# Up projections of two MLPs: two of four pairs of input row tiles by seven products of sums

## The chip, the cores and the metric

The kernel runs on one core of one Trainium2 chip. The metric is the device time in microseconds (us) of one execution, for fixed inputs of the sizes below. Outputs are compared with the reference's.

## The reference

A two-layer trunk over 1056 frames: 1024 of a new stream (the prompt) and 32 of a running one (the sample). The model width is 1024, the MLP's is 4096, and all data are float32.

```
for i in range(2):
    a = rmsnorm(h, norm_mix[i])
    y = hgrn2_mixer(a, ...) if i == 0 else short_conv_mixer(a, ...)
    h = h + y
    m = rmsnorm(h, norm_mlp[i])
    h = h + square(relu(m @ w_up[i])) @ w_down[i]     # (1056,1024)@(1024,4096), (1056,4096)@(4096,1024)
return rmsnorm(h, norm_final), states
```

The change is in the MLP, in the output projections of the two mixers ahead of it (`y @ w_out`, 1024 by 1024) and in how the weights of the conv mixer are cut.

## The kernel before, in words

Data lie transposed: the 1024 channels as eight tiles of 128 partitions by 1056 tokens (`hT[0]` to `hT[7]`). Every float32 operand is split into a high part (a cast to the matmul's fp32r, on ScalarE: `xh`, `whi`) and a low part (the operand less its high part, on VectorE: `xl`, `wlo`). A product is three matmuls, low by high, high by low and high by high (`mm3`), into one PSUM sum. A scale of a norm is applied where a product is read (`nrm.r`, made by `Norm.scale` with nine VectorE operations over 1056 columns, `rsqrt`), the norm's vector where the operand is split.

An MLP runs over 16 chunks of 256 of its 4096 columns:

- `up(c, 0)` and `up(c, 1)` make the chunk's two row tiles `u`: eight input tiles, tokens in groups of 384, 384 and 288, three matmuls each: 72 matmuls a stage. VectorE reads PSUM by relu times scale (L787), ScalarE squares (L788).
- `sums(c)` takes the two tiles `u` as a matrix of two by two blocks (two row tiles by two halves of 528 tokens) and makes from it seven factors B11, Q1, Q2, B22, T3, B21, T4 (`xsums`): four sums and differences on VectorE, each factor with a high part on ScalarE and a low part on VectorE.
- `down(c, 0)` and `down(c, 1)` multiply these by seven factors of the down weights A11, S1, S2, S4, S3, A12, A22, for two pairs `p` of output tiles each: seven products of two by two blocks where plain multiplication has eight. A product is six matmuls of 264 columns (three, by two quarters of the tokens); a stage is 7 x 2 x 6 = 84 matmuls (L812). S1 to S4 are sums of weight blocks, made by four additions on POOL in the raw tile (L720), after A11, A12 and A22 have been cast from it. Products gather in PSUM banks named a, b and c, and each gathered value is also added to the right half of an `hT` tile: by VectorE (L821), and in steps 0 and 6 (`STAGED`) by a copy to SBUF on ScalarE (`st`, L708) and an addition on POOL (L709). A bank is used again after it is read.

The stages come as up(c,0), up(c,1), down(c-1,0), down(c-1,1), sums(c). The weights of a stage are loaded and cut two stages ahead. Within that, a scheduler sets each engine's own order; an engine does its list strictly in that order. PSUM has four tiles (`pb`) of two banks. In layer 1 the last two chunks are multiplied plainly at the end (`groups`), in layer 0 the last one (`plain`).

Where the words below speak of a chunk, it is one up part and two down stages: in the steady part of the trace one follows the other every 43.9 us.

Of the kernel before, what the change touches and what calls it, by code (L numbers as in the profile page):

```python
# [8 lines left out]
F32 = mybir.dt.float32  # L9
# [26 lines left out]
def trunk_kernel(  # L36
# [21 lines left out]
    xs = ctx.enter_context(tc.tile_pool(name="xs", bufs=1))  # L58
    ws = ctx.enter_context(tc.tile_pool(name="ws", bufs=4))
    fp = ctx.enter_context(tc.tile_pool(name="fp", bufs=18))  # L60
    pj_cm = tc.tile_pool(name="pj", bufs=3, space=PSUM)
# [13 lines left out]
    xh = [xs.tile([P, NTOK], F32R, tag=f"xh{k}", name=f"xh{k}") for k in range(KT)]  # L75
    xl = [xs.tile([P, NTOK], F32R, tag=f"xl{k}", name=f"xl{k}") for k in range(KT)]
# [509 lines left out]
    for steps in late:  # L586
        steps()
    hp_cm.__exit__(None, None, None)
    for k in range(KT):
        split(k, heads[k].Y)  # L590
    rc_cm.__exit__(None, None, None)
    pj_cm.__exit__(None, None, None)


    mp = ctx.enter_context(tc.tile_pool(name="mp", bufs=1, reuse_waits="tile"))
    pb = ctx.enter_context(tc.tile_pool(name="pb", bufs=4, space=PSUM, reuse_waits="tile"))

# [10 lines left out]
    def mm_block(ps, n, c0, wt, j, srcs, kk0=0):  # L608
        nk = len(srcs)
        cs = slice(j * P, (j + 1) * P)  # L610
        for k in range(nk):
            hi, lo = wt[(kk0 + k) // 4]
            kk = (kk0 + k) % 4
            ah, al = srcs[k]
            mm3(ps[:, :n], hi[:, kk, cs], lo[:, kk, cs], ah[:, c0 : c0 + n], al[:, c0 : c0 + n],
                k == 0, k == nk - 1)

    def mm_rows(pss, wt, j, srcs, mid=None):

        cs = slice(j * P, (j + 1) * P)  # L620
        nk = len(srcs)
        for k in range(nk):
            hi, lo = wt[k // 4]
            ah, al = srcs[k]
            if mid and k == nk - 1:
                mid()
            for g in range(3):
                sl, n = gsl(g)
                mm3(pss[g][:, :n], hi[:, k % 4, cs], lo[:, k % 4, cs], ah[:, sl], al[:, sl], k == 0, k == nk - 1)

    xsrc = [(xh[k], xl[k]) for k in range(KT)]
    hT = [None] * KT

    class Norm:


        def __init__(self):
            self.acc = mp.tile([P, NTOK], F32, tag="acc", name="acc")
            self.n = 0

        def add(self, m):
            if self.n == 0:
                nc.scalar.activation(self.acc, hT[m], AF.Square)
            else:
                sq = mp.tile([P, NTOK], F32, tag="sq", name="sq")
                nc.scalar.activation(sq, hT[m], AF.Square)
                nc.gpsimd.tensor_tensor(self.acc, self.acc, sq, op=ALU.add)
            self.n += 1

        def scale(self):  # L650
            v = mp.tile([P, NTOK], F32, tag="sq", name="nv")
# [10 lines left out]
    def out_proj(W, first):  # L662

        nrm = Norm()
        for m2 in range(4):
            wt = wload(W, m2)
            for j in range(2):
                m = 2 * m2 + j
                if first:
                    hT[m] = ft(f"hT{m}")  # L670
                    nc.gpsimd.dma_start(out=hT[m], in_=x_t[m * P : (m + 1) * P, :])
                _, pss = trio()
                if m in (0, KT - 1):
                    mm_rows(pss, wt, j, xsrc)
                for g in range(3):
                    sl, n = gsl(g)
                    ps = pss[g]
                    if 0 < m < KT - 1:
                        mm_block(ps, n, sl.start, wt, j, xsrc)
                    nc.vector.tensor_tensor(hT[m][:, sl], hT[m][:, sl], ps[:, :n], op=ALU.add)  # L680
                nrm.add(m)
        return nrm

    def split_h(k, vcol):
        split(k, hT[k], scale=vec[:, vcol + k : vcol + k + 1])
# [10 lines left out]
    WAT = {"A11": (0, 0), "A12": (0, 1), "A22": (0, 2), "S2": (1, 0), "S4": (1, 1), "S1": (1, 2), "S3": (1, 3)}  # L696
# [4 lines left out]

    TO = (((0, 0, ALU.add),), ((1, 1, ALU.subtract),), ((0, 1, ALU.add),), ((0, 1, ALU.add),),
          ((1, 1, ALU.subtract),), ((0, 0, ALU.add),), ((1, 0, ALU.subtract),))
    q2 = lambda t: t.rearrange("p (i c) -> p i c", i=2)
    STAGED = (0, 6)

    def stage(d, st, v, op):
        nc.scalar.copy(q2(st), v)  # L708
        nc.gpsimd.tensor_tensor(d, d, st, op=op)  # L709

    def wsums(src):

        raw, hi, lo = wtiles()
        hi2 = ws.tile([P, 4, 256], F32R, tag="whi", name="whi")
        lo2 = ws.tile([P, 4, 256], F32R, tag="wlo", name="wlo")
        nc.sync.dma_start(out=raw, in_=src)
        nc.scalar.copy(hi[:, :3], raw[:, :3])
        nc.vector.tensor_tensor(lo[:, :3], raw[:, :3], hi[:, :3].bitcast(F32), op=ALU.subtract)  # L718
        for d, o in ((2, 3), (3, 0), (0, 2), (1, 0)):
            nc.gpsimd.tensor_tensor(raw[:, d], raw[:, d], raw[:, o], op=ALU.add)  # L720
        nc.scalar.copy(hi2, raw)
        nc.vector.tensor_tensor(lo2, raw, hi2.bitcast(F32), op=ALU.subtract)
        ts = ((hi, lo), (hi2, lo2))

        def at(f, p):
            t, i = WAT[f]
            return [x[:, i, p * P : (p + 1) * P] for x in ts[t]]

        return at

    def xsums(u0, u1):
# [4 lines left out]
        def part(f, src, neg=False):  # L736
            t = fp.tile([P, 2, HALF], F32R, tag="ft", name=f)
            h, l = t[:, 0], t[:, 1]
            if neg:
                nc.scalar.activation(h, src, AF.Copy, scale=-1.0)  # L740
                nc.vector.scalar_tensor_tensor(l, src, -1.0, h.bitcast(F32), op0=ALU.mult, op1=ALU.subtract)
            else:
                nc.scalar.copy(h, src)
                nc.vector.tensor_tensor(l, src, h.bitcast(F32), op=ALU.subtract)
            X[f] = (h, l)

        add = lambda d, a, b, op: nc.vector.tensor_tensor(d, a, b, op=op)
        part("B11", b11)
        part("B22", b22)
        add(b22, b12, b22, ALU.subtract)  # L750
        add(b12, b11, b12, ALU.subtract)
        add(b11, b22, b11, ALU.subtract)
        part("Q1", b12)
        part("Q2", b11)
        part("T3", b22, True)
        part("B21", b21)
        add(b21, b11, b21, ALU.add)
        part("T4", b21, True)
        return X

    def mlp(layer, nrm, on_final, last):
        Wu, Wd = wg_up[layer], wg_down[layer]
        U, X = {}, {}
        two = lambda t: t[:, :768].rearrange("p (i c) -> p i c", i=2)
        sq = lambda t: nc.scalar.activation(t, t, AF.Square)

        def up(c, j):
            m = 2 * c + j

            def run(wt):  # L770
# [357 lines left out]
```

## Time and profile before

| what | value |
|---|---|
| time, median of 3 runs | 2445.47 us (2443.81 to 2446.0) |
| the profiled execution | 2445.29 us, span 2443.6 us, granted clock 0.995 |
| busy TensorE, VectorE, ScalarE, GpSimd | 2412.2, 1635.0, 775.8, 744.1 us |
| HBM traffic | 114 MB read, 5 MB written, 49 GB/s |
| HGRN mixer up to its output projection | 0 to 527 us of the span |
| output projection, MLP of layer 0 | 527 to 620, 620 to 1343 us |
| conv mixer, MLP of layer 1 | 1343 to 1710, 1710 to 2443 us |

PE is TensorE's matmuls, PEld its weight loads, DVE VectorE, ACT ScalarE, POOL GpSimd. A row of the timeline has the start, the length, the engine, the line, output and inputs with their shape, how many instructions stand together, and in brackets the idle time before them and what ended it. A row of the chain of waits has the start, the length, and the engine, tile and line. A row of a group has the busy time and the mean length of one instruction in ns. Lines are those of the kernel before.

### The profile page before, as it was taken

What the parts mean: (1) busy time and instruction counts of PE and PEld (TensorE: products, weight loads), DVE (VectorE), ACT (ScalarE), POOL (GpSimd) and SP (SyncE); (2) the same over time, 40 slices, a digit from 0 to 9 for tenths busy, and PEclk for the clock granted to TensorE, in tenths of its full rate; (3) what the DMA queues carried; (4) which work ended last, traced back from release to release, by engine and by line L of the source; (5) the groups of instructions that cost most, each with busy time, mean ns of one, the idle gap of its engine ahead of it and who ended that gap; (6) DMA issues with size and microseconds to landing.
All of it is one profiled execution on the core that took longest, in us unless ns stands there. A gap on an engine that the chain in (4) does not pass through costs nothing.

```text
span 2443.6 us, 39446 instructions
## 1 busy us (share of the span) xinstructions
PE 2412.2 (99%) x16548; PEld 2373.4 (97%) x16548; DVE 1635.0 (67%) x2384; ACT 775.8 (32%) x1275; POOL 744.1 (30%) x792
## 2 busy tenths in 40 slices
PE   8999999999999999999999999999999999999998
PEld 8999999989999999999999999999999999999997
DVE  8776666652887787877868533343877877868765
ACT  5121212122433334333335111023334333333334
POOL 3110100102244453444545000002253444534423
PEclk9999999999999999999999999999999999999999
DMA  4101010121011111111111111111111111111111
GB/s 151 39 21 56 22 56 22 56 91 52 28 60 44 45 51 44 61 44 44 53 44 54 42 52 44 43 53 36 41 47 44 61 44 44 53 44 61 44 35 71
DMA packets 35760, 121.99 MB, mean 50 GB/s; under 512 B 4336, under 2 KB 7552, under 8 KB 35584
## 3 DMA queue, kind: packets, MB, share of 16 engines
q1 hardware_dynamic: 33632, 113.58, 14.4%
q0 software_dynamic: 1952, 5.92, 0.7%
q8 instruction: 129, 2.11, 0.4%
q14 instruction: 47, 0.39, 0.1%
HBM read 114.09 MB, written 5.39 MB: 49 GB/s over the span
## 4 chain that ended last, share of the span: by engine, by line
PE 97%; DVE 2%; ACT 0%; issue 0%; DMA 0%; DVEq 0%; SPq 0%; ACTq 0%
PE pb L812 25%; PE pb L108 17%; PE pb L109 17%; PE pb L110 17%; PE pj L108 4%; PE pj L109 4%; PE pj L110 3%; PE v L492 1%; PE v L493 1%; PE v L494 1%; PE aps L385 1%; PE aps L390 1%; PE ops L427 1%; PE ups L402 1%; PE ops L426 1%; PE aps L388 0%
## 5 line engine op out<-in xcount | busy, mean ns | idle before, releaser
L108 PE MATMUL pb<-xh,wlo 128*128 128x384 f32 (+1 forms) x2544 | 829.3, 326 | 3.4 <-DVE hT L838 3.4
L109 PE MATMUL pb<-xl,whi 128*128 128x384 f32 (+1 forms) x2544 | 822.4, 323 | 0.0
L110 PE MATMUL pb<-xh,whi 128*128 128x384 f32 (+1 forms) x2544 | 822.4, 323 | 0.0
L709 POOL TENSOR_TENSOR hT<-hT,st 128x528 f32<-128x528 f32 x232 | 373.2, 1635 | 404.0 <-ACT st L708 404.0
L108 PEld LDWEIGHTS pb<-xh,wlo 128*128 128x128 f32 x2544 | 478.6, 188 | 8.2 <-issue 2.5
L110 PEld LDWEIGHTS pb<-xh,whi 128*128 128x128 f32 x2544 | 478.7, 188 | 0.4
L109 PEld LDWEIGHTS pb<-xl,whi 128*128 128x128 f32 x2544 | 478.7, 188 | 0.2
L821 DVE TENSOR_TENSOR hT<-hT,pb 128x528 f32<-128x528 f32 x580 | 383.4, 697 | 9.1 <-PE pb L812 0.8
L720 POOL TENSOR_TENSOR raw<-raw 128x256 f32<-128x256 f32 x232 | 209.7, 904 | 336.5 <-DVE wlo L718 322.8
L94 ACT CAST whi<-raw 128x1024 fp32r<-128x1024 f32 (+1 forms) x143 | 149.0, 1044 | 454.9 <-PE pb L110 268.0
L95 DVE TENSOR_TENSOR wlo<-raw,whi 128x1024 fp32r<-128x1024 f32 (+1 forms) x143 | 202.6, 1420 | 67.4 <-ACT whi L94 66.9
L812 PE MATMUL pb<-B,whi 128*128 128x264 f32 x1392 | 226.8, 285 | 0.0
L812 PEld LDWEIGHTS pb<-B,whi 128*128 128x128 f32 x1392 | 193.2, 189 | 0.0
L108 PE MATMUL pj<-xh,wlo 128*128 128x384 f32 (+1 forms) x536 | 177.7, 332 | 7.1 <-ACT xh L183 7.1
L109 PE MATMUL pj<-xl,whi 128*128 128x384 f32 (+1 forms) x536 | 173.4, 323 | 0.0
L110 PE MATMUL pj<-xh,whi 128*128 128x384 f32 (+1 forms) x536 | 173.1, 323 | 0.0
L787 DVE SCALAR_TENSOR_TENSOR u<-pb,nr 128x768 f32<-128x768 f32 x120 | 82.2, 704 | 124.0 <-PE pb L110 124.0
L708 ACT COPY st<-pb 128x528 f32<-128x528 f32 x232 | 133.0, 600 | 80.6 <-PE pb L812 68.9
L812 PE MATMUL pb<-T,whi 128*128 128x264 f32 x928 | 150.9, 284 | 0.0
L812 PE MATMUL pb<-Q,whi 128*128 128x264 f32 x928 | 150.7, 284 | 0.0
L812 PE MATMUL pb<-B,wlo 128*128 128x264 f32 x696 | 144.6, 289 | 3.3 <-DVE hT L821 3.3
L788 ACT ACTIVATE u<-u 128x768 f32<-128x768 f32 (+1 forms) x128 | 81.7, 642 | 161.3 <-DVE u L787 156.4
(243 smaller groups left out, 3620.3 us busy)
## 6 DMA issues: line engine op xcount, KB each, us to landing
raw<-in_wg_up_dram SPq DMA_DIRECT2D x64, 512.0 KB, 3.5
raw<-in_wg_down_dram SPq DMA_DIRECT2D x64, 512.0 KB, 3.5
raw<-in_wg_in_hgrn_dram SPq DMA_DIRECT2D x31, 512.0 KB, 4.3
raw<-in_wg_cu_conv_dram SPq DMA_DIRECT2D x16, 512.0 KB, 3.5
xk<-in_x_t_dram SPq DMA_DIRECT2D x8, 528.0 KB, 8.6
hT<-in_x_t_dram POOLq DMA_DIRECT2D x8, 528.0 KB, 7.3
raw<-in_wg_out_hgrn_dram SPq DMA_DIRECT2D x8, 512.0 KB, 4.1
raw<-in_wg_b_conv_dram SPq DMA_DIRECT2D x8, 512.0 KB, 3.6
```

Source lines behind the costliest of these rows:

```text
L94: nc.scalar.copy(hi, raw)
L95: nc.vector.tensor_tensor(lo, raw, hi.bitcast(F32), op=ALU.subtract)
L108: nc.tensor.matmul(ps, wlo, ah, start=start, stop=False)
L109: nc.tensor.matmul(ps, whi, al, start=False, stop=False)
L110: nc.tensor.matmul(ps, whi, ah, start=False, stop=stop)
L708: nc.scalar.copy(q2(st), v)
L709: nc.gpsimd.tensor_tensor(d, d, st, op=op)
L720: nc.gpsimd.tensor_tensor(raw[:, d], raw[:, d], raw[:, o], op=ALU.add)
L787: nc.vector.scalar_tensor_tensor(d, ps, 0.0, rr, op0=ALU.max, op1=ALU.mult)
L788: nc.scalar.activation(u[:, sl], u[:, sl], AF.Square)
L812: nc.tensor.matmul(t[:, q, :QT], wf, xf[:, q * QT : (q + 1) * QT], start=start and n == 0, stop=n == 2, skip_group_check=True)
L821: nc.vector.tensor_tensor(q2(d), q2(d), v, op=op)
```

## The change

The up projection of a chunk becomes one stage `up(c)`. Input row tiles 0 to 3 are taken as two pairs, and each pair's product with the chunk's two output tiles goes by seven products, as the down stages do it; tiles 4 to 7 stay plain, in halves of 528 tokens. The stage is 7 x 2 x 6 + 4 x 4 x 6 = 180 matmuls of 264 columns. Its list is `PAIR`: the bank, the two factors (or the output tile and half, for the plain products) and the name of the read that follows. Eight reads of PSUM gather the four blocks of `u` in SBUF: the first of a block is a copy by ScalarE or, for the last block, a read by VectorE together with the scale; the others are additions on VectorE. The second output tile is made with its sign turned (`op0` is min, and its plain weights are scaled by -1). The first chunk of a layer uses the order `LATE`, with the norm's scale made ahead of its step 10, and scales after all reads.

The up weights come as two tiles of 1024 columns (`wpair`): one is cut as the down weights are, with four additions on POOL, one into two plain parts. Weight parts are tiles of 512 columns, six for the high and six for the low parts, where there were four of 1024; raw tiles are two, not three. The factors of the input tiles are made once a layer: `hsums` in `out_proj`, after output tiles 3 and 5. They share the tiles of `xh` and `xl` or lie in six tiles `e`. The staged copies of the down stages have two tiles, not four.

```diff
-    def out_proj(W, first):
+    def out_proj(W, first, xsrc, vcol):
...
+            if m in (3, 5):
+                X = hsums(m // 2 - 1, X, vcol)
+        X["rows"] = [parts(hT[k], vec[:, vcol + k : vcol + k + 1]) for k in range(4, KT)]
+        return nrm, X
...
-    WAT = {"A11": (0, 0), "A12": (0, 1), "A22": (0, 2), "S2": (1, 0), "S4": (1, 1), "S1": (1, 2), "S3": (1, 3)}
+    WAT = {"A11": (0, 0), "A12": (0, 2), "A22": (1, 0), "S1": (2, 0), "S3": (2, 2), "S2": (3, 0), "S4": (3, 2)}
...
     def wsums(src):
 
-        raw, hi, lo = wtiles()
-        hi2 = ws.tile([P, 4, 256], F32R, tag="whi", name="whi")
-        lo2 = ws.tile([P, 4, 256], F32R, tag="wlo", name="wlo")
-        nc.sync.dma_start(out=raw, in_=src)
-        nc.scalar.copy(hi[:, :3], raw[:, :3])
-        nc.vector.tensor_tensor(lo[:, :3], raw[:, :3], hi[:, :3].bitcast(F32), op=ALU.subtract)
+        raw = wraw(src)
+        t = lambda i: raw[:, i * 256 : (i + 1) * 256]
+        hl = [wpart(raw[:, :512]), wpart(t(2))]
         for d, o in ((2, 3), (3, 0), (0, 2), (1, 0)):
-            nc.gpsimd.tensor_tensor(raw[:, d], raw[:, d], raw[:, o], op=ALU.add)
-        nc.scalar.copy(hi2, raw)
-        nc.vector.tensor_tensor(lo2, raw, hi2.bitcast(F32), op=ALU.subtract)
+            nc.gpsimd.tensor_tensor(t(d), t(d), t(o), op=ALU.add)
+        hl += [wpart(raw[:, 512:]), wpart(raw[:, :512])]
...
+    def mm_half(ps, wt, x, start, stop):
+        hi, lo = wt
+        for n, (w, v) in enumerate(((lo, x[0]), (hi, x[1]), (hi, x[0]))):
+            for q in range(2):
+                nc.tensor.matmul(ps[:, q, :QT], w, half(v, q), start=start and n == 0, stop=stop and n == 2,
+                                 skip_group_check=True)
+    PAIR = (("a", ("A11", "B11"), "a1"), ("b", ("S1", "Q1"), "b1"), ("c", ("A12", "B21"), None), ("c", (0, 0), "c"),
+            ("a", ("S2", "Q2"), "a2"), ("d", (1, 1), "d"), ("a", ("S3", "T3"), "a3"), ("b", ("S4", "B22"), None),
+            ("b", (0, 1), "b2"), ("a", ("A22", "T4"), None), ("a", (1, 0), "a4"))
+    LATE = (0, 1, 4, 7, 6, 2, 9, 3, 8, 10, 5)
+    def wpair(src):
+        at = wsums(src[0])
+        raw = wraw(src[1])
+        return at, wpart(raw[:, :512]), wpart(raw[:, 512:], -1.0)
...
+    READ = {"a1": (0, 0), "c": (0, 0), "a2": (0, 1), "b2": (0, 1), "b1": (1, 1), "a3": (1, 1), "d": (1, 1), "a4": (1, 0)}
...
+                    if b in made:
+                        nc.vector.tensor_tensor(q2(d), q2(d), ps, op=ALU.add)
+                    elif left[b] or c == 0:
+                        nc.scalar.copy(q2(d), ps)
+                    else:
+                        src = ps
+                    made.add(b)
+                    if not left[b]:
+                        r = lambda: nrm.r[:, sl]
+                        def end():
+                            if src is d:
+                                nc.vector.scalar_tensor_tensor(d, d, 0.0, r(), op0=op0, op1=ALU.mult)
+                            else:
+                                nc.vector.scalar_tensor_tensor(q2(d), src, 0.0, q2(r()), op0=op0, op1=ALU.mult)
+                            nc.scalar.activation(d, d, AF.Square)
+                        later.append(end) if c == 0 else end()
```

How the change moves instructions is seen in the order of three engines. The number behind a name tells tiles of one name apart; `st` is a staged copy, `raw` a weight tile as loaded, `pb` a PSUM tile.

GpSimd (POOL), in a steady part of layer 0, the two down stages before the next up stage. Before, the last six staged additions of the pair of downs, and the weights' additions (of the down stages of the next chunk) behind them:

```order
L709 TENSOR_TENSOR hT1_5399<-hT1_5399,st_21448 128x528
L709 TENSOR_TENSOR hT3_5575<-hT3_5575,st_21457 128x528
L709 TENSOR_TENSOR hT4_5669<-hT4_5669,st_21473 128x528
L709 TENSOR_TENSOR hT6_5845<-hT6_5845,st_21483 128x528
L709 TENSOR_TENSOR hT5_5751<-hT5_5751,st_21566 128x528
L709 TENSOR_TENSOR hT7_5927<-hT7_5927,st_21575 128x528
L720 TENSOR_TENSOR raw_21603<-raw_21603 128x256 x4
```

Now, the same six (L894) with the four additions of the next up stage's weights, raw_12478 (L740), in between:

```order
L894 TENSOR_TENSOR hT1_5427<-hT1_5427,st_12610 128x528
L894 TENSOR_TENSOR hT3_5611<-hT3_5611,st_12619 128x528
L740 TENSOR_TENSOR raw_12478<-raw_12478 128x256
L894 TENSOR_TENSOR hT4_5732<-hT4_5732,st_12651 128x528
L740 TENSOR_TENSOR raw_12478<-raw_12478 128x256
L894 TENSOR_TENSOR hT6_5945<-hT6_5945,st_12661 128x528
L740 TENSOR_TENSOR raw_12478<-raw_12478 128x256 x2
L894 TENSOR_TENSOR hT5_5824<-hT5_5824,st_12744 128x528
L894 TENSOR_TENSOR hT7_6037<-hT7_6037,st_12753 128x528
```

st_12610 and st_12619 are the last step of the first down, st_12651 and st_12661 the first step of the second.

VectorE (DVE) in the second of the two down stages. Before, only reads of PSUM stand together from step 1 to step 5 (pb_16549 and pb_16559 are the banks a of the two pairs):

```order
L821 TENSOR_TENSOR hT4_5669<-hT4_5669,pb_16569 128x528
L821 TENSOR_TENSOR hT6_5845<-hT6_5845,pb_16577 128x528
L821 TENSOR_TENSOR hT5_5751<-hT5_5751,pb_16549 128x528
L821 TENSOR_TENSOR hT7_5927<-hT7_5927,pb_16559 128x528
L821 TENSOR_TENSOR hT4_5669<-hT4_5669,pb_16627 128x528
```

Now, with the low parts of the up stage's summed weights (L598) among them:

```order
L896 TENSOR_TENSOR hT4_5732<-hT4_5732,pb_12664 128x528
L896 TENSOR_TENSOR hT6_5945<-hT6_5945,pb_12672 128x528
L598 TENSOR_TENSOR wlo_12493<-raw_12478,whi_12492 128x512
L896 TENSOR_TENSOR hT5_5824<-hT5_5824,pb_12644 128x528
L598 TENSOR_TENSOR wlo_12497<-raw_12478,whi_12496 128x512
L896 TENSOR_TENSOR hT7_6037<-hT7_6037,pb_12654 128x528
L896 TENSOR_TENSOR hT4_5732<-hT4_5732,pb_12722 128x528
```

wlo_12497 needs all four additions of raw_12478; the stage's last product, T4 of the second pair, goes into pb_12654 again.

ScalarE (ACT) at the start of layer 0's MLP, the factors of chunk 0 and what follows them. Before, the squares of chunk 1's first row tile, in SBUF, come behind them:

```order
L740 ACTIVATE T3_6247<-u_6225 128x528
L743 CAST B21_6250<-u_6225 128x528
L740 ACTIVATE T4_6254<-u_6225 128x528
L717 CAST whi_6351<-raw_6350 128x768
L788 ACTIVATE u_6345<-u_6345 128x768
```

Now the first copies of up(1) out of PSUM come behind them (L848; pb_6493 is bank a):

```order
L600 ACTIVATE T3_6459<-u_6223 128x528
L597 CAST B21_6462<-u_6223 128x528
L600 ACTIVATE T4_6466<-u_6223 128x528
L848 COPY u_6491<-pb_6493 128x528
L848 COPY u_6492<-pb_6507 128x528
```

In the later chunks these two copies also stand behind T4 of the chunk before.

More of the change, by code (lines that the diff above doesn't have):

```diff
@@ L729, in wsums, with xsums @@
         return at
-    def xsums(u0, u1):
+    def xsums(u0, u1, new):
         b11, b12, b21, b22 = u0[:, :HALF], u0[:, HALF:], u1[:, :HALF], u1[:, HALF:]
         X = {}
[L736 to L741, printed above, removed]
-            else:
[L743 to L759, printed above, removed]
@@ L900, in mlp @@
             stages.append(down(n - 1, 0))
-            stages.append(lambda: [split(6 + j, U[n][j]) for j in range(2)])
+            stages.append(lambda: [gsplit(u, et) for u in U[n]])
             stages += [down(n - 1, 1), plain(0), plain(1)]
@@ L1002, in trunk_kernel @@
+        nc.gpsimd.dma_start(out=s_conv, in_=zs.rearrange("p j m -> p (j m)"))
+        xsrc = [parts(ys[k]) for k in range(KT)]
+    nrm, X = out_proj(wg_out_conv, False, xsrc, V_NMLP + 8)
     fin = {}
```

459 lines of the change are left out of this document (244 added, 215 removed).

## The prediction

> **What bounds the kernel now.** I read the page first: the share of each engine, then the chain that ended last.
>
> ```profile
> span 2443.6 us, 39446 instructions
> PE 2412.2 (99%) x16548; PEld 2373.4 (97%) x16548; DVE 1635.0 (67%) x2384; ACT 775.8 (32%) x1275; POOL 744.1 (30%) x792
> ...
> PE 97%; DVE 2%; ACT 0%; issue 0%; DMA 0%; DVEq 0%; SPq 0%; ACTq 0%
> ```
>
> TensorE is busy for 99% of the span and is 97% of the chain. So a matmul saved is time saved, and any new wait of TensorE adds in full: no slack elsewhere could give it back. The chain's longest pieces give the price of one chunk of the MLP, and TensorE's timeline gives the pace of the two matmul widths.
>
> ```profile
> 887.79 20.65 PE pb L812 x168
> 931.67 20.69 PE pb L812 x168
> ```
>
> ```profile
> 908.28 0.33 PE L108 MATMUL pb<-xh,wlo 128*128 128x384 f32 x1
> ...
> 916.70 0.29 PE L108 MATMUL pb<-xh,wlo 128*128 128x288 f32 x1
> ```
>
> From one pair of down stages to the next is 43.88 us. The 168 matmuls of 264 columns take 20.65, that is 0.1229 each; the 144 of the up stages take the other 23.23. In these, 48 matmuls of 384 columns stand between 908.28 and 916.70: 0.1754 each, which leaves 0.133 for one of 288.
>
> How late may a read of PSUM be before TensorE stops? The waits show one such place, and VectorE's timeline explains it.
>
> ```profile
> PE pb L812 <- DVE hT L821: 3.3, 2, 2.3
> ```
>
> ```profile
> 1292.90 0.70 DVE L821 TENSOR_TENSOR hT<-hT,pb 128x528 f32<-128x528 f32 x1
> 1293.52 2.15 DVE L181 TENSOR_TENSOR xl<-u,xh 128x1056 fp32r<-128x1056 f32 x1
> 1295.59 2.35 DVE L95 TENSOR_TENSOR wlo<-raw,whi 128x1024 fp32r<-128x1024 f32 x1
> 1297.86 2.53 DVE L821 TENSOR_TENSOR hT<-hT,pb 128x528 f32<-128x528 f32 x4
> ```
>
> Two low parts of 4.5 us ran on VectorE ahead of a read of PSUM, and TensorE waited 2.3 us. In a down stage the product that uses a bank again comes 18 matmuls after the one that has to be read, 18 x 0.1229 = 2.2 us. VectorE need not be full to stop TensorE: one late instruction ahead of a read is enough.
>
> **The change, part by part.**
>
> *Fewer columns.* An up stage of a chunk has 180 matmuls of 264 columns, in the same form as the down stages' (one weight for two halves), instead of 96 of 384 and 48 of 288. At the down row's pace that is 180 x 0.1229 = 22.13 us against 23.23: 1.1 us less, and over 32 chunks **-35 us**. Split into a part per column and a part per matmul, the rows (264: 0.1229, 384: 0.1754) give 0.4375 ns a column and 7.4 ns a matmul: 3168 columns fewer save 1.39 us, 36 matmuls more cost 0.27. The gain is gone if the fixed part is over 38 ns.
>
> The Trainium skill speaks against this: its page "TensorE: Matmul & The Clock Gate", section "Back-to-back issue gap", gives 81 ns for a matmul of 128 columns and 131 ns for 512 in a stream with weight loads. By a line through these (an estimate from that page) an up stage would go from 15.9 to 17.8 us, 61 us worse in all. The rows above disagree: 384 columns take 175 ns here, more than the page's 512. I go by the rows.
>
> *A wait in the second down stage.* The change puts four additions of weight parts on POOL for the up stage, and the rows of the order show where they stand: between the staged additions of the downs, because the part for A22 must be cast before the first addition and its tile comes free only at the end of the first down. On VectorE the last summed low part (wlo_12497) stands ahead of the read of pb_12654 into hT7. So that read, which TensorE's last step waits for, now hangs on all of POOL's chain. The durations, from POOL, ScalarE and VectorE:
>
> ```profile
> 889.84 2.84 POOL L709 TENSOR_TENSOR hT<-hT,st 128x528 f32<-128x528 f32 x2 [4.09 <-ACT st L708]
> 897.98 6.18 POOL L709 TENSOR_TENSOR hT<-hT,st 128x528 f32<-128x528 f32 x4 [5.30 <-ACT st L708]
> ...
> 912.23 4.34 POOL L720 TENSOR_TENSOR raw<-raw 128x256 f32<-128x256 f32 x4
> 926.46 3.19 POOL L720 TENSOR_TENSOR raw<-raw 128x256 f32<-128x256 f32 x4 [9.90 <-DVE wlo L718]
> ```
>
> ```profile
> 897.30 1.33 ACT L708 COPY st<-pb 128x528 f32<-128x528 f32 x2 [1.13 <-PE pb L812]
> ...
> 912.86 0.64 ACT L743 CAST Q<-u 128x528 fp32r<-128x528 f32 x1 [3.74 <-DVE u L747]
> ```
>
> ```profile
> 901.61 5.61 DVE L821 TENSOR_TENSOR hT<-hT,pb 128x528 f32<-128x528 f32 x9
> 907.14 0.69 DVE L744 TENSOR_TENSOR B<-u,B 128x528 fp32r<-128x528 f32 x1
> ```
>
> Let T be the start of the two downs (887.79 above). The first down's last staged copy begins at T + 9.5 (897.30) and POOL at T + 10.2 (897.98), as now. From there POOL has four staged additions of 1.42 to 1.55 (2.84/2, 6.18/4) and four of weights of 0.80 to 1.09 (3.19/4, 4.34/4): 8.9 to 10.5 us. I take 1.55, which is this very place, and 0.80, since the slower row ran beside VectorE's 1.5 us operations: 9.4, so T + 19.6. Then the cast, the low part and the read of hT7: nine additions in 5.61 us show that 0.70 us records follow each other every 0.62, so 0.57 + 0.62 + 0.62 and the read is done at T + 21.4. TensorE wants it after 162 matmuls, T + 19.9. Stall 1.5 us, from 1.0 to 2.6 by the other ends. It can't be below nothing, as no step of a down stage gets shorter. 28 stages have this order (14 pairs of downs of each layer that an up follows): 28 x 1.5 = **+42 us** (28 to 73). In the kernel before POOL's weight additions stood behind all staged ones and no read waited for them.
>
> Two tiles for the staged copies, where there were four, come near as well: the second copy of the second down needs POOL's second addition (T + 13.3), so ends at T + 13.9, and TensorE wants that bank after 114 matmuls, T + 14.0. It costs nothing by these rows; what POOL loses more would be in the same stall.
>
> *A wait in the up stage.* On ScalarE the copy of the stage's first block out of PSUM (L848) stands behind T4's high part, the end of the sums of the chunk before; TensorE needs that bank again after 73 matmuls, 9.0 us into the stage. From the stage's start, VectorE has one low part, four additions of halves and four low parts of factors before T4, and another low part of weights. Alone and beside POOL these take:
>
> ```profile
> 908.37 0.70 DVE L747 TENSOR_TENSOR u<-u 128x528 f32<-128x528 f32 x1
> 908.99 2.08 DVE L718 TENSOR_TENSOR wlo<-raw,whi 128x768 fp32r<-128x768 f32 x1
> 910.99 3.00 DVE L747 TENSOR_TENSOR u<-u 128x528 f32<-128x528 f32 x2
> ...
> 925.42 0.96 DVE L718 TENSOR_TENSOR wlo<-raw,whi 128x768 fp32r<-128x768 f32 x1 [1.27 <-ACT whi L717]
> ```
>
> The low part can start 0.75 us in, after its cast. These ten operations at 0.62 to 0.65 each, with two waits of 0.1, end at 7.2, T4's cast and the copy at 8.4: no wait. POOL has two staged additions in the first 3 us, and the rows show what VectorE loses beside it: 2.08 against 0.96, 1.5 against 0.70. One or two losses of 0.7 give a copy at 9.1 to 9.8; a loss on every operation of those 3 us, 2 us and more, gives 11. I take 0.5 us of stall, from 0 to 2, in 27 stages: **+13 us** (0 to 54). The Trainium skill, page "SBUF — State Buffer", section "SBUF: two separate sides", says that a VectorE operation on two SBUF inputs and a GpSimd operation lock each other out for a whole instruction. The rows agree as to the pair of engines, with 0.8 to 1.1 us lost on an operation; a whole addition lost once, 1.42 us, would give a copy at 9.8 and a stall of 0.8.
>
> *A wait at the layer's start.* The norm's scale is made inside up(0), after 132 matmuls: 16.2 us into it. What hangs on it is long, and the trace has its length at the same place of the kernel before:
>
> ```profile
> 629.98 1.13 PE pb L656 x4
> ...
> 631.46 0.73 PE pb L656 x2
> ```
>
> ```profile
> 646.40 1.26 DVE L140 SCALAR_TENSOR_TENSOR nr<-acc,nr 128x1056 f32<-128x1056 f32 x1
> 647.69 2.56 DVE L784 TENSOR_TENSOR u<-u,nr 128x768 f32<-128x768 f32 x4
> ```
>
> ```profile
> 658.58 0.65 ACT L740 ACTIVATE T<-u 128x528 fp32r<-128x528 f32 x1 [1.68 <-DVE u L747]
> ```
>
> From the norm's matmuls to the scale 17.7 us, from there to T4's high part 11.6 us (659.23). The order on ScalarE puts up(1)'s first copy behind that T4 (it stood before as T4 ahead of up(1)'s squares, which TensorE did not wait for), so the copy ends at 16.2 + 17.7 + 11.6 + 0.6 = 46.1 us after up(0)'s start. TensorE is through up(0) at 24 (180 matmuls and the norm's 1.9 us) and wants the bank 84 matmuls into up(1), at 34.3. Stall 11.8; the sums' order has fewer large low parts in between than before, 1 us less: I take 11, from 8 to 13. Two layers: **+22 us** (16 to 26).
>
> *The rest.*
>
> ```profile
> 928.52 0.96 DVE L787 SCALAR_TENSOR_TENSOR u<-pb,nr 128x768 f32<-128x768 f32 x1 [2.14 <-PE pb L110]
> ...
> 931.71 0.46 DVE L787 SCALAR_TENSOR_TENSOR u<-pb,nr 128x288 f32<-128x288 f32 x1 [1.50 <-PE pb L110]
> ```
>
> VectorE has eight reads and scalings of 0.7 for two of 0.96 and two of 0.46, and 768 columns of low parts more: from 33.5 of 43.88 (the sum of its busy times in that stretch) to about 37, POOL from 19.8 to 23. By sums neither is full.
>
> ```profile
> sum 43.88, PE 43.88 PEld 43.70 DVE 33.48 ACT 16.37 POOL 19.83; mean PE 10.97 PEld 10.92 DVE 8.37 ACT 4.09 POOL 4.96
> ```
>
> The factors of the inputs are made in out_proj, beside 11.6 us of matmuls for an output tile (1056 columns of eight products: 24 x 0.1754 x 2 + 24 x 0.133), on ScalarE and VectorE, for 3 us a tile. Without that cover they would cost about 20 us a layer. The HGRN part keeps its order, and a chunk loads as many bytes as before, two stages ahead; TensorE waits for no load now. Smaller weight parts should end some of the 2.3 us stall shown above: **-2 us** (0 to -6).
>
> Sum: -35 + 42 + 13 + 22 - 2 = +40. The profiled execution took 2445.29 us (span 2443.6), 0.2 under the median of 2445.47; so **2485 us**. All low ends give 2448, all high ones 2564.
>
> **Rivals.** *The waits of the chunks are not there*: POOL is through by T + 18.1 and up's copy in time. For it: VectorE is idle for 10 of 43.88 us, and the first wait is a small difference of times near 20 us. Against: even POOL's fastest rows end at T + 19.1. Then -35 + 22 - 2 = 2430 us, and 2408 if the layer's start is covered too: faster. Chance 0.15. *The stall is there at a third of its size* (0.5 us in 28 stages): -35 + 14 + 22 - 2, 2444 us, no change. Chance 0.08. *VectorE becomes the bound*: beside 23 us of POOL its 37 us stretch by the 1.2 to 2.2 times of the rows above; with 8 us more, 45.3 a chunk against TensorE's 42.8, that is 2.5 x 28 + 22 = 2537 us. Against: it has held 33.5 of 43.88 beside 19.8. Chance 0.05. *The weight loads come into the open.* Each of the 36 added matmuls brings a load:
>
> ```profile
> L812 PEld LDWEIGHTS pb<-B,whi 128*128 128x128 f32 x1392 | 193.2, 189 | 0.0
> ```
>
> Unhidden, 36 x 0.189 less the 1.39 us of columns is 5.4 us more a chunk, and with the stalls 2445 + 173 + 75 = 2693 us. Against: 168 loads stand hidden behind matmuls in 20.65 us of the same form. Chance 0.02. By the estimate from the Trainium skill's page on TensorE, above, this rival would be 2445 + 61 + 75 = 2581 us.
>
> **How the numbers follow.** The three waits as worked out hold 0.70, with 2450 to 2530 as their own range. The range of 2440 to 2530 leaves out the first rival and the two last ones. A measurement of this kernel can tell about 0.2% from no change, 4.9 us. Faster: 0.16; the same: 0.08; slower: 0.76.
>
> **What would show it.** Right: waits of TensorE for VectorE's hT at the down's line, about 28 of 1 to 2.6 us; for ScalarE's u at the read's line about 27 short ones and two near 11 us, some 10 us after the first up of a layer; 180 matmuls of an undisturbed up in 22.1 us. Wrong: those lines missing in the waits, POOL's last weight addition before T + 18, or an up stage with gaps between its matmuls.

## The result and the profile after

The changed kernel takes 2527.05 us (median of 4 runs, 2524.48 to 2527.96) against 2444.64 us for the kernel before (4 runs): 1.0336 times as long, with an interval of 1.0318 to 1.0354. It is 82 us slower, where 40 had been forecast. The profiled execution has a span of 2524.4 us, 80.8 more than before.

The page of the changed kernel, its first lines: TensorE is busy for 95% of the span instead of 99%, with 16 us less of work, and VectorE for 131 us more.

```profile
span 2524.4 us, 42862 instructions
PE 2395.7 (95%) x17700; PEld 2337.3 (93%) x17700; DVE 1766.0 (70%) x2834; ACT 921.0 (36%) x1679; POOL 786.9 (31%) x920
```

TensorE's waits in the changed kernel (engine, line, what it waited for, then us in total, times, the longest). Before, no line of this list for the MLPs had more than 3.4 us in total.

```profile
PE pb L790 <- ACT u L848: 63.7, 31, 11.2
PE pb L790 <- DVE hT L896: 30.2, 57, 1.8
PE pj L114 <- ACT xh L189: 6.4, 1, 6.4
PE pb L114 <- DVE wlo L598: 5.8, 1, 5.8
```

The first line is the copy of the up stage's blocks out of PSUM: two waits of 11.2 us at the layers' starts, 27 of 1.4 to 1.5 in the later up stages and two of 1.1 in the layers' first ones. The second is the down stages'. TensorE's own timeline over one chunk shows where they stand; in brackets is the listed wait.

```profile
791.69 0.51 PE L790 MATMUL pb<-B,wlo 128*128 128x264 f32 x2 [0.81 <-DVE hT L896]
...
796.84 0.51 PE L790 MATMUL pb<-T,wlo 128*128 128x264 f32 x2 [0.22 <-DVE hT L896]
...
808.20 0.51 PE L790 MATMUL pb<-Q,wlo 128*128 128x264 f32 x2 [1.45 <-ACT u L848]
```

The same three stand in every chunk. The next chunk has the first of them at 837.80, so a chunk takes 46.11 us where it took 43.88. The first is step B22 of the second down stage, the second its step T4, the third the up stage's second use of bank a. The listed time is not all: from one matmul's start to the next, 1.07, 0.74 and 1.71 us are over the usual pace at and around these places, 3.5 us where 2.48 are listed.

### The profile page after: what moved, and what is told of

Its sections match the earlier page's. It is cut to its first block, busy times and chain, and to the rows that moved or that the text cites. A ratio compares the mean times of both kernels' runs of the same rounds, so it can differ in the third digit from the quotient of the medians.

```text
span 2524.4 us, 42862 instructions
## 1 busy us (share of the span) xinstructions
PE 2395.7 (95%) x17700; PEld 2337.3 (93%) x17700; DVE 1766.0 (70%) x2834; ACT 921.0 (36%) x1679; POOL 786.9 (31%) x920
## 5 line engine op out<-in xcount | busy, mean ns | idle before, releaser
L597 ACT CAST whi<-raw 128x512 fp32r<-128x512 f32 (+1 forms) x476 | 275.2, 579 | 771.4 <-PE pb L116 285.9
L740 POOL TENSOR_TENSOR raw<-raw 128x256 f32<-128x256 f32 x360 | 300.2, 834 | 596.8 <-DVE wlo L598 584.7
L598 DVE TENSOR_TENSOR wlo<-raw,whi 128x512 fp32r<-128x512 f32 (+1 forms) x476 | 329.3, 693 | 136.6 <-ACT whi L597 135.1
L894 POOL TENSOR_TENSOR hT<-hT,st 128x528 f32<-128x528 f32 x232 | 338.7, 1471 | 192.5 <-ACT st L893 192.5
L114 PE MATMUL pb<-xh,wlo 128*128 128x384 f32 (+1 forms) x960 | 311.0, 324 | 5.8 <-DVE wlo L598 5.8
L115 PE MATMUL pb<-xl,whi 128*128 128x384 f32 (+1 forms) x960 | 310.5, 323 | 0.8 <-DVE xl L601 0.8
L116 PE MATMUL pb<-xh,whi 128*128 128x384 f32 (+1 forms) x960 | 311.1, 324 | 0.0
L790 PE MATMUL pb<-xh,wlo 128*128 128x264 f32 x1024 | 214.3, 286 | 0.0
L790 PE MATMUL pb<-xh,whi 128*128 128x264 f32 x1024 | 208.4, 285 | 0.0
L790 PE MATMUL pb<-xl,whi 128*128 128x264 f32 x1024 | 208.2, 285 | 0.0
L790 PEld LDWEIGHTS pb<-Q,whi 128*128 128x128 f32 x1440 | 201.7, 190 | 0.0
L114 PEld LDWEIGHTS pb<-xh,wlo 128*128 128x128 f32 x960 | 180.9, 188 | 6.2 <-issue 5.9
```

Source lines behind the costliest of these rows:

```text
L114: nc.tensor.matmul(ps, wlo, ah, start=start, stop=False)
L115: nc.tensor.matmul(ps, whi, al, start=False, stop=False)
L116: nc.tensor.matmul(ps, whi, ah, start=False, stop=stop)
L740: nc.gpsimd.tensor_tensor(t(d), t(d), t(o), op=ALU.add)
L790: nc.tensor.matmul(ps[:, q, :QT], w, half(v, q), start=start and n == 0, stop=stop and n == 2, skip_group_check=True)
```

## The experiments

Line numbers are those of the kernel that a listing belongs to; one line may differ by some ten from kernel to kernel. A high part is an operation of ScalarE, a low part one of VectorE. The edits are shortened to the lines that matter; `...` stands for lines left out, and the words behind `#` are added here. `behind(x, y)` puts x after y in its engine's order.

### T4 behind the copies

From chunk 1 on, the factor T4 is made after the next up stage has copied a1 and b1.

```diff
-        fac("T4", b21, -1.0)
+            last.append(lambda: fac("T4", b21, -1.0))     # in xsums; the list is held in up
...
                         seen[what] = nc.scalar.copy(q2(d), ps)
+                        if what == "b1" and held:
+                            held.pop()()
```

> Only the factor T4 of a chunk is made after the next up stage's copies of its first two blocks (a1, b1) on ScalarE, from chunk 1 on; the layers' starts stay as they are. Theory of the order: each of the 27 up waits (1.43 us listed, and 0.26 more until the matmuls are at their pace again) goes, 27 x 1.7 = 46 us, so about 2481 us, and TensorE's waits for ScalarE's u fall from 63.7 us to about 22 (the two layer starts). Rival, VectorE is the bound (36.7 us busy of a chunk's 46.1, each operation in its way): TensorE waits for the next read instead, the time falls by less than 12 us.

Measured: 2505.45 us, 1.0244 of before [1.0214, 1.0274], so 22 us under the changed kernel, half of what the theory of the order gave. The wait is shorter, not gone: in a chunk 0.66 us are left of 1.45. The first line of the waits, then ScalarE's copies and TensorE's product in one up stage, which starts at 797.88:

```profile
PE pb L800 <- ACT u L858: 41.8, 31, 11.2
```

```profile
805.35 1.09 ACT L858 COPY u<-pb 128x528 f32<-128x528 f32 x2
```

```profile
805.99 0.51 PE L800 MATMUL pb<-Q,wlo 128*128 128x264 f32 x2 [0.66 <-ACT u L858]
```

ScalarE's copy no longer stands behind T4, but still behind B21's cast and a weight cast, which come as late as VectorE lets them. But more than T4 moved here: the scheduler also set TensorE's order anew, and the product that needs the bank now comes after 60 matmuls of the up stage instead of 73. The first copy ends about 8.0 us into the stage, where it ended 10.4 us in; against the old place, 9.0 us in, it would be in time. By these times the half that is left comes from TensorE asking earlier; the run doesn't show that moving T4 alone would have been too little.

### B22 behind its read

```diff
+                            if i == 1:
+                                seen["rd"] = rd                   # down: the reads of step S1, Q1
...
+            if rd:
+                behind(seen["B22"][1], rd)        # sums: VectorE's low part of B22 after that read
```

> VectorE's low part of the factor B22 stands behind the read of the second pair's Q1 product instead of ahead of it, nothing else moves. The wait at the step B22 of the second down stage (0.8 us listed, 1.07 in all, 28 times) goes in any case. If POOL's chain decides how early the last summed weight part is there, TensorE only comes sooner to the wait at step T4, which grows from 0.7 to about 1.5 us: 0.3 x 28 = 8 us less, 2519 us. If the two waits are independent: 30 us less, 2497 us.

Measured: 2529.75 us, 1.0343 [1.0313, 1.0374]: no gain, so neither figure came, though the wait moved as the theory of POOL's chain had it. TensorE's waits for the down stages, and one of them:

```profile
PE pb L797 <- DVE hT L906: 29.2, 29, 1.8
```

```profile
799.79 0.51 PE L797 MATMUL pb<-T,wlo 128*128 128x264 f32 x2 [0.98 <-DVE hT L906]
```

29 waits where there were 57, with the same sum: step B22 has none now, and step T4 has 0.98 us instead of 0.22. TensorE came sooner to the place where it had to wait anyway. What VectorE waits for ahead of that read, in this kernel:

```profile
797.78 1.14 ACT L597 CAST whi<-raw 128x512 fp32r<-128x512 f32 x2 [2.45 <-POOL raw L747]
```

```profile
798.43 0.69 DVE L598 TENSOR_TENSOR wlo<-raw,whi 128x512 fp32r<-128x512 f32 x1 [0.67 <-ACT whi L597]
```

Here POOL's chain sets the end: the cast waits for POOL's last addition, and VectorE for the cast. In the changed kernel the same three places read

```profile
792.85 1.56 POOL L740 TENSOR_TENSOR raw<-raw 128x256 f32<-128x256 f32 x2
```

```profile
794.44 0.62 ACT L597 CAST whi<-raw 128x512 fp32r<-128x512 f32 x1 [1.05 <-POOL raw L740]
```

```profile
795.50 0.68 DVE L598 TENSOR_TENSOR wlo<-raw,whi 128x512 fp32r<-128x512 f32 x1
```

There the cast is done at 795.06 and VectorE comes to the low part at 795.50 without a pause: it has been at work since B22's low part, which started late (789.67, below). So in the changed kernel VectorE's own run is the last to end, and POOL's chain is 0.4 us ahead of it; take VectorE's out of the way and POOL's is there.

### The summed weights behind their read

```diff
+                            if b and i == 4 and p and c < NFC - 2 and "w4" in seen:   # the second pair's T3 read
+                                behind(seen.pop("w4")[1], rd)     # VectorE: low part of S2, S4 after it
```

> VectorE's low part of the last summed weight part (S2, S4) of the up stage stands behind the read of the second pair's T3 product instead of ahead of it, nothing else moves. The wait at step T4 (0.74 us in all, 28 times) goes: 21 us less, 2506 us. Rival: the part before it (S1, S3), which stays ahead of the other pair's read, and the casts keep VectorE as late: less than 7 us faster.

Measured: 2524.10 us, 1.0320 [1.0290, 1.0350]: 3 us less, a miss for the first theory. Step T4's second wait is no longer in the list, but gaps of 0.1 to 0.2 us over the pace remain there and at the next up stage's first product, and the up stage's wait went from 1.45 to 1.66 us: TensorE was 0.2 us sooner there and VectorE was not. Here too the time went to the next place where TensorE waits.

### The norm earlier

```diff
-                    mm_pair(w, X, read, LATE, {10: nrm.scale})
+                    mm_pair(w, X, read, LATE, {9: nrm.scale1, 3: nrm.scale2})   # two token groups, then the third
```

> The norm's scale of a layer's first up stage is made in two pieces, after 72 and 84 of its 180 matmuls instead of after 132. Theory: the stall of 11.2 us in up(1) hangs on the scale and its factors, which come 6 to 7 us sooner: stall about 4.5 us per layer, and the clock drop behind it (2 us per layer) smaller: 14 to 18 us less, 2509 to 2513 us. Rival: the sum of squares is not ready and TensorE waits at the new place, or the factors of chunk 0 wait for something else than the scale: within 4 us of 2527.

Measured: 2526.42 us, 1.0330 [1.0300, 1.0360]: nothing. TensorE's waits show both halves of the expectation at once:

```profile
PE pb L806 <- ACT u L864: 53.7, 29, 7.3
...
PE pb L687 <- POOL acc L682: 6.5, 2, 3.3
```

The stall in up(1) fell from 11.2 to 7.3 us, and TensorE now waits 3.3 us for the sum of squares, which is not ready at the new place. 10.6 in all: the path from the sum of squares through the scale to the factors and the copy is nearly as long as before, and it makes no difference where on it TensorE waits.

### The copies ahead of all sums

From chunk 1 on, everything of the sums after B22 (the three differences, Q1, Q2, T3, B21, T4) is written behind the next up stage's copies of a1 and b1.

```diff
         fac("B22", b22)
-        add(nc.vector, b22, b12, b22, ALU.subtract)
-        ...
-        fac("T4", b21, -1.0)
+        held.append(rest)       # rest() does these; up's read of "b1" calls it
```

> The sums of a chunk's factors from Q1 on (and the three sums ahead of them) are written behind the next up stage's copies of a1 and b1, from chunk 1 on; the layers' starts and the down stages stay. The run with T4 alone behind the copies gave half of what its wait is worth, with 0.66 us of wait left behind ScalarE's other parts, which wait for VectorE; VectorE works there without a pause for 17 us. Theory: TensorE waits only because the copy stands behind that work, so with the copies ahead of it the whole wait goes, 27 x 1.7 = 46 us, about 2481 us, and VectorE catches up in its pauses later in the stage. Rival: VectorE's backlog passes to its own reads of PSUM in the up stage, waits for VectorE's u appear, and the time stays at 2500 us or above.

Measured: 2479.44 us, 1.0143 [1.0122, 1.0163]: 47.6 us under the changed kernel, as the theory said. TensorE's waits:

```profile
PE pb L797 <- DVE hT L907: 30.4, 56, 1.8
PE pb L797 <- ACT u L855: 24.5, 4, 11.2
```

Of the waits for the copies only the layers' starts are left; the down stages' stand as they were, and no new wait for VectorE's u appears. TensorE asks for the bank after 60 matmuls here too, and finds it read. A chunk takes 44.35 us.

### What VectorE loses beside POOL

Left out: POOL's additions of the last step of each second down stage, so that these products don't reach the output. All orders stay.

```diff
-                            nc.gpsimd.tensor_tensor(d, d, st, op=op)
+                            if i == 0 or b == 0:
+                                nc.gpsimd.tensor_tensor(d, d, st, op=op)
```

> POOL's two additions of the last step of each second down stage are left out (these products don't reach the output), so POOL does nothing in the first 13 us of the up stage; every engine's order is the changed kernel's. In the changed kernel the copy that TensorE waits for in the up stage ends 10.4 us in, where the prediction had 8.4 without a loss beside POOL: the three sums of halves took 3.3 us there, the low part before them 1.2. Theory: this loss beside POOL is the mis-sized term; the copy comes at about 8.4 to 8.9, the wait goes but for what is left of 9.0: 2485 to 2495 us. Rival: VectorE's amount of work, or ScalarE's parts in between, sets the copy: the wait stays above 1 us and the time above 2510.

Measured: 2480.35 us, 1.0150 [1.0121, 1.0180]: 46.7 us less, 5 us under the range of the theory. VectorE's timeline, the changed kernel's up stage (which starts at 797.68) first, then this kernel's (from 795.05):

```profile
798.54 1.20 DVE L601 SCALAR_TENSOR_TENSOR wlo<-raw,whi 128x512 fp32r<-128x512 f32 x1
799.67 3.32 DVE L759 TENSOR_TENSOR u<-u 128x528 f32<-128x528 f32 x3
```

```profile
795.91 0.69 DVE L601 SCALAR_TENSOR_TENSOR wlo<-raw,whi 128x512 fp32r<-128x512 f32 x1
796.52 2.19 DVE L759 TENSOR_TENSOR u<-u 128x528 f32<-128x528 f32 x3
```

And POOL beside the first of them, then ScalarE's copies in the changed kernel and in this one:

```profile
797.38 3.55 POOL L894 TENSOR_TENSOR hT<-hT,st 128x528 f32<-128x528 f32 x2 [2.98 <-ACT st L893]
```

```profile
807.02 0.64 ACT L600 ACTIVATE T<-u 128x528 fp32r<-128x528 f32 x1 [1.77 <-DVE u L759]
807.57 1.08 ACT L848 COPY u<-pb 128x528 f32<-128x528 f32 x2
```

```profile
803.29 1.08 ACT L848 COPY u<-pb 128x528 f32<-128x528 f32 x2
```

Without POOL's two additions the same four VectorE operations take 2.8 us from the first's start to the last's end instead of 4.5, and the copy begins 8.2 us into the stage instead of 9.9. TensorE wants its result 9.0 us in. So the wait of 1.7 us in each up stage is what VectorE loses beside two POOL additions, passed on whole because the copy stands behind that work; to take away either, the loss here or the order in the run before, is enough.

### POOL's additions for the up weights

Left out: the four additions for the up weights; their S1 to S4 are then plain blocks.

```diff
-        at = wsums(src[0])
+        at = wsums(src[0], False)      # wsums without its four additions
```

> The four additions on POOL are left out for the up weights alone (their S1 to S4 are then plain blocks, so this kernel computes other up products); the order of all else is the changed kernel's. The run with B22 behind its read showed the wait of the second down stage move from step B22 to step T4 and keep its sum of 1.8 us. If POOL's chain sets that end, step T4's wait goes (0.74 us, 28 times, 21 us less) and what VectorE loses beside POOL with it; step B22's wait, which hangs on the second staged addition and the two staged tiles ahead of it, stays at 0.5 to 1.07: 2490 to 2506 us. If VectorE's own amount of work sets it: within 8 us of 2527.

Measured: 2499.30 us, 1.0221 [1.0191, 1.0251]: 28 us less, inside the range for POOL's chain, but not where it was expected.

```profile
PE pb L790 <- DVE hT L896: 11.0, 54, 0.7
```

```profile
790.93 0.51 PE L790 MATMUL pb<-B,wlo 128*128 128x264 f32 x2 [0.17 <-DVE hT L896]
...
795.82 0.51 PE L790 MATMUL pb<-T,wlo 128*128 128x264 f32 x2 [0.23 <-DVE hT L896]
```

Step T4 keeps its 0.23 us, step B22 falls from 0.81 to 0.17. VectorE's low part of B22 tells why; the changed kernel, POOL at that place, and this kernel:

```profile
789.67 1.35 DVE L598 TENSOR_TENSOR B<-u,B 128x528 fp32r<-128x528 f32 x1 [1.08 <-ACT B L597]
```

```profile
790.42 1.19 POOL L740 TENSOR_TENSOR raw<-raw 128x256 f32<-128x256 f32 x1
```

```profile
789.55 0.71 DVE L598 TENSOR_TENSOR B<-u,B 128x528 fp32r<-128x528 f32 x1 [1.08 <-ACT B L597]
```

VectorE waits the same 1.08 us for it, since B22's cast stands on ScalarE behind a staged copy, and that copy waits for POOL to free one of the two staged tiles:

```profile
788.51 0.60 ACT L893 COPY st<-pb 128x528 f32<-128x528 f32 x1 [0.87 <-POOL hT L894]
789.00 0.64 ACT L597 CAST B<-u 128x528 fp32r<-128x528 f32 x1
```

What the additions cost is above all this operation's length, 1.35 against 0.71, on which VectorE's unbroken run behind it hangs. They account for 0.9 us of the 1.8 in a chunk; the other 0.9 stay without any of them, so for that half the late start of B22's low part is what the rows show. More staged tiles, as the kernel before had, were not tried.

### The layer's start

Scaling, squares and factors of chunk 0 are written behind up(1)'s copies of a1 and b1.

```diff
-                for f in later:
-                    f()
+                held.append(lambda: [f() for f in later])     # for c == 0; sums(0) is held too
```

> Scaling, squares and factors of chunk 0 of a layer are written behind up(1)'s copies of a1 and b1; the later chunks stay. The run with the earlier norm showed the sum of squares as the limit of that path, so the order is what is left. Theory of the order: the waits of 11.2 us go in both layers, and the low clock after them (2 us a layer): 2497 to 2505 us. Rival: the path from the sum of squares to the factors limits the start anyway, and TensorE waits as long for VectorE's reads in up(1) or for the factors in down(0, 0): above 2518 us.

Measured: 2509.25 us, 1.0265 [1.0244, 1.0285]: 17.8 us less, between the two ranges and nearer the first. The 11.2 us are gone; in their place stand short waits in up(1) and the downs behind it, 3.7 us per layer:

```profile
672.72 0.51 PE L797 MATMUL pb<-Q,wlo 128*128 128x264 f32 x2 [0.88 <-ACT st L912]
674.91 0.48 PE L797 MATMUL pb<-Q,wlo 128*128 128x264 f32 x2 [0.95 <-DVE u L853]
678.42 0.51 PE L797 MATMUL pb<-B,wlo 128*128 128x264 f32 x2 [1.32 <-DVE hT L915]
683.81 0.48 PE L797 MATMUL pb<-T,wlo 128*128 128x264 f32 x2 [0.55 <-DVE hT L915]
```

The path of the norm, which could not be made shorter by an earlier start, was kept out of TensorE's way by order.

### All waits of the chunks

The copies first, as above; in the second down stage B22's low part and both low parts of the summed up weights behind the reads; and the up stage in the order A11, A12, first plain product, S1.

```diff
-    PAIR = (("a", ("A11", "B11"), "a1"), ("b", ("S1", "Q1"), "b1"), ("c", ("A12", "B21"), None), ("c", (0, 0), "c"),
+    PAIR = (("a", ("A11", "B11"), "a1"), ("c", ("A12", "B21"), None), ("c", (0, 0), "c"), ("b", ("S1", "Q1"), "b1"),
```

> As the run with the copies first, and besides in the second down stage: VectorE's two low parts of the summed up weights stand behind the last read that TensorE waits for there, B22's low part behind the read of Q1's product, and the up stage starts with A11, A12 and the first plain product, so that it needs the first summed weights 5.9 us in instead of 1.5. Theory: POOL's chain is late only against what TensorE asks of it; all waits of the chunks go, 28 x (1.7 + 1.7): about 2431 us. Rival: POOL's chain and VectorE's backlog show as waits for the summed weights in the up stage: 2480 us.

Measured: 2446.06 us, 1.0006 [0.9996, 1.0017]: 81 us less, no different from the kernel before. Neither theory's number: no wait for summed weights is left, and the second line below has 1.6 us where 30.2 stood, but 15 us of what was hoped for are not there.

```profile
PE pb L805 <- ACT u L864: 24.6, 4, 11.2
...
PE pb L805 <- DVE hT L918: 1.6, 2, 1.0
```

A chunk takes 43.10 us, where 348 matmuls at 0.1229 are 42.77 and 46.11 less the 3.5 us of waits 42.6. The rest stands as gaps of 0.1 to 0.25 us over the pace at the steps that use a bank again, with no wait listed; what makes them was not tried.

### All orders, and the kernel that beats both

The run before with the layer's start, and the first weights of the output projection taken first (their low parts stood behind four low parts of the inputs on VectorE, TensorE's wait of 5.8 us above). The second run has the changed kernel's own order of products again.

```diff
-            wt = wrow(W[m])
+            if m: wt = wrow(W[m])
+            else:
+                with tc.high_priority(): wt = wrow(W[m])
```

> The run before with the order of the layer's start as well, and the first weights of the first output projection ahead of the low parts of its inputs on VectorE (5.8 us of wait). Theory of the order: 2431 less 26 less 7, about 2398 to 2405 us, 40 us below the kernel before: the columns' gain whole. Rival: 2440 us or above, some wait is left that no order removes.

> The run with all orders, but the up stage's own order is the changed kernel's again: A11, then S1, which asks for the first summed weights 1.5 us into the stage instead of 5.9. If POOL's additions and the low parts behind them are late in themselves, TensorE waits there 0.5 to 1.0 us in 28 stages: 2437 to 2451 us. If it was only their place ahead of the reads: 2423 us, within 5.

Measured: 2423.20 us, 0.9914 of before [0.9898, 0.9931], and 2422.65 us, 0.9907 [0.9879, 0.9936]. Both are 104 us under the changed kernel and 22 under the kernel before, with the change's arithmetic and its tiles untouched: only the orders differ. The first missed the theory's 2398 to 2405 by about 20 us: 15 are the run before's, and the layers' starts keep some, since the first full period of a layer is about 48.2 us instead of 43.1. The second came out at the 2423 expected if only the place was at fault. The two runs are alike, so the summed weights are not late in themselves, even 1.5 us into the stage; they were only in the way.

## Why the prediction was right or wrong

The direction and the three places were right, the size was not: 82 us against 40.

- **Fewer columns, -35 us.** Right: an up stage without waits takes 22.0 us in the runs with the copies ahead (22.13 worked out, 23.23 before). The best order has 43.10 us a chunk against 43.88, 0.8 of the 1.1; 0.3 us stay in the short gaps.
- **The wait in the second down stage, +42 us.** The size was about right: 1.07 + 0.74 us in 28 stages are 51 us, and the orders of the run with all waits of the chunks give back 33 of them (from 2479 to 2446; the up stage's own order, which that run also changed, makes no difference by the last two runs). The times were right as well: counted from T, the start of the two downs (775.24 in the chunk shown), POOL's last addition ends at T + 19.2 (19.6 worked out) and TensorE goes on at T + 21.6 (the read done at 21.4). The cause that was named is half of it: without the four additions 28 us go and the rest stays. Not named was that most of the wait shows at step B22, for which two things are late: a cast behind a staged copy that waits for one of two staged tiles, and a low part that takes twice its time beside POOL. From there VectorE's own run reaches the last read 0.4 us behind POOL's chain. That two chains end so near each other made the size right; that part is luck. The working had looked at these two tiles, but only for the bank they free, not for what is queued behind the copy on ScalarE.
- **The wait in the up stage, +13 us: the step that failed.** It said that ten operations end at 7.2 us, and charged "one or two losses of 0.7" beside POOL: 0.5 us of stall. Measured are 1.7 us in each of 27 stages, 46 us; the copies ahead of the sums give back 47.6 us, and POOL's two additions left out give back 46.7. Alone, the chain is what was worked out (the copy ends 8.8 us in against 8.4). The loss beside POOL was 1.6 us on four operations, not 0.7 on one or two, and its other end, "2 us and more", stood in the text and was not taken. This one term is 33 us of the 42 that are missing.
- **The wait at the layer's start, +22 us.** Right: 11.2 us in each layer, 11 predicted. Both ends of it came about 2 us later than worked out (the copy ends 47.4 us after up(0)'s start and TensorE wants the bank at 36.1, against 46.1 and 34.3), which the difference does not show. The 2 us of half pace behind each wait (last section) were not in the sum. The other order gives back 18.
- **The rest, -2 us.** 5.8 us at the first output projection were not foreseen: smaller weight parts did not help there, as they stand behind four low parts of the inputs. The MLP of layer 0 starts 2.0 us later than before (621.64 against 619.64).
- **What is left over.** The terms as measured, -39 (32 up stages of 22.0 against 23.23), +51, +46, +22, +4 for the half pace and +2, add to 86 us, where 82 were measured. The 4 us were not followed.
- **The rivals.** Waits that are not there, and a stall of a third: wrong, as the listed waits show. VectorE as the bound: wrong as it was meant (36.7 of 46.1 us busy in a chunk, about 37 worked out), and yet near to the truth for 17 us of each chunk, in which it worked without a pause and two single orders only moved the wait to its next place. Weight loads in the open: wrong, as an up stage of 180 matmuls without waits takes 22.0 us.

The estimate from the Trainium skill's page "TensorE: Matmul & The Clock Gate", section "Back-to-back issue gap" (81 ns for 128 columns, 131 ns for 512), put the changed up stage above the old one. The runs disagree: 264 columns take 122 to 123 ns here, and fewer columns are a gain.

## What to carry to other kernels

An engine works through its list in order, so a read of PSUM is as late as the slowest operation ahead of it on its engine, with all that this one waits for; of a new stage, ask of each read what stands ahead of it. Take a wait away and look where it goes: three single edits here gained 3 us or less, as TensorE waited elsewhere for the same work; the one that took the read out of that work's line gained 48, the whole set 104. And a term that is the small difference of two long chains should be charged with the losses that the same operations already show beside their neighbour, at the full number of operations.

## What the runs showed of the hardware

After a wait of 11.2 us TensorE ran at half its pace for 4.6 us: 20 matmuls of 264 columns at 0.22 us each, then 0.12 again. That is 2 us more for each such wait. The mean granted clock of the execution is 0.990 with these two waits, 0.996 in the run that reorders the layers' starts and 0.995 before.

```profile
669.13 0.81 PE L790 MATMUL pb<-Q,wlo 128*128 128x264 f32 x2 [11.19 <-ACT u L848]
669.74 1.08 PE L790 MATMUL pb<-Q,whi 128*128 128x264 f32 x4
...
673.26 0.64 PE L790 MATMUL pb<-B,wlo 128*128 128x264 f32 x2
...
674.61 0.41 PE L790 MATMUL pb<-T,wlo 128*128 128x264 f32 x2
```

The Trainium skill's page "TensorE: Matmul & The Clock Gate", section "What's actually happening", has a clock of a half after an idle window of about 3.4 us and full speed after as much sustained work; these rows agree in kind, with 4.6 us at half pace here. The waits of 0.2 to 1.7 us show no slow matmuls behind them.

A short wait costs more than its listed time: 0.81 us listed are 1.07 from start to start, 1.45 are 1.71, since the modelled end of the matmul ahead covers 0.16 (it is listed with 0.28 at a pace of 0.12) and the first matmuls after the wait are together 0.1 over their pace. For the 88 waits of the first two lines of the list that is up to 23 us which the list does not have.
